# Residual norms of a two-model block stack taken token tile by token tile

## The chip, the cores and the metric

One core of one Trainium2 chip runs the program. The metric is the device time of one execution in microseconds (us), the median over several executions. The engines are called TensorE (PE; PEld is its weight load), VectorE (DVE), ScalarE (ACT), GpSimd (POOL) and SyncE (SP, which issues the transfers).

## The reference

Two models run one after the other on 256 tokens of width 1024 in fp32, two layers each. The first is a conditioned block with three mixers and a convolutional feed-forward network; its output x is the second one's input. The second model is the one whose norms are changed:

```python
for l in range(DEPTH):                                   # DEPTH = 2
    h = rms_norm_2(x, norm_mix_pre[l])
    (c_q, c_kv, k_rope, ..., gate_logits) = split(h @ w_in[l], pts)
    y_a = mla_branch(c_q, c_kv, k_rope, ...) @ w_o_mla[l]  # norms c_q and c_kv first
    ...
    merged = g[:, :, 0] * y_a + g[:, :, 1] * y_b + g[:, :, 2] * y_c + g[:, :, 3] * y_d
    x = x + rms_norm_2(merged @ w_out[l], norm_mix_post[l])
    h2 = rms_norm_2(x, norm_ffn_pre[l])
    f_g, f_u = split(h2 @ w_ffn_in[l])
    f = (silu(f_g) * f_u) @ w_ffn_out[l]
    x = x + rms_norm_2(f, norm_ffn_post[l])
```

`rms_norm_2(x, g)` divides each row by the root of its mean square (plus 1e-6) and multiplies by g. So a residual of the second model takes two norms in a row: of the product that is added, and of the sum for the next product.

## The kernel before

The 256 tokens are two token tiles t0 and t1 of 128 rows. A product's weights come from memory in pieces of 128x1024 fp32 (`raw`), and `weights` splits each piece into a high half `wh` (a cast on ACT, L259) and a low half `wl` (a subtraction on DVE, L260). Every product is three matmuls (`mm3`, L178 to L180): high by high, high by low, low by high. Activations are split in the same way (L262 on ACT, L263 on DVE when a gain is applied). A scheduler decides in which order each engine's instructions stand; each engine then works strictly in that order. `queue` adds an order without a wait for data. The table `HOLD` says, per norm ("site"), how many weight pieces may be split freely before the norm's last splits and how many stand behind them.

The second model has five places at which a residual ends: gpre of layer 0 (the first model's feed-forward product `down`, L868, gated and added, then normed as input of layer 0), gffn of layer 0 (product with w_out, `out_proj`, L1240), gpre of layer 1 (product with w_ffn_out, `down`, L1325), gffn of layer 1, and the end, where x goes out (L1399). The four accumulators of such a product, two halves cc of 512 columns for each token tile, lie in PSUM banks named acc, acc (t0) and ada, o (t1). The product runs in groups of two row blocks: for each group t0's four products (two row blocks by two halves), then t1's.

`add_normed` (L1350) takes the sums of squares of all four halves on ACT (L216), multiplies by the gain (L1361, DVE), computes the reciprocal root per token tile (`rsqrt`, L189 to L202, small DVE steps), adds to x (L1366, DVE, twice per tile) and sums the squares of the new x on ACT. `normed` (L219) takes the second reciprocal root, scales x (L232 on DVE for the left half, L233 on ACT for the right) and transposes it on PE, eight 128x128 blocks per token tile (L236), into four banks that both token tiles share; `norm_split` then splits the transposed blocks.

Behind gpre come the latent products (`lat`, banks acc, 24 matmuls of 512 columns per token tile), the product of the rope key (`krp`, 48 matmuls of 256 columns), the latents' own norm (sums of squares on ACT, a four-column Newton chain L189, L207 to L211 and scalings L1027 on DVE), its transposes (L1034, PE) and the rope key's own steps L1014 and L1015 (DVE). Behind gffn comes the feed-forward network: 22 hidden tiles of 128, each with 48 matmuls of 256 columns (weights stationary, tokens moving), Silu on ACT (L1339) and a product on DVE (L1340), and every two hidden tiles one group of `down`.

## Time and profile before

| what | value |
|---|---|
| median of 3 runs | 2169.36 us (2168.35 to 2172.04) |
| the profiled execution's own time | 2168.22 us |
| its span in the trace | 2166.4 us |
| PE busy | 2081.5 us, 96% of the span, 14228 matmuls |
| DVE busy | 1493.9 us, 69% |
| ACT busy | 1075.5 us, 50% |
| read from HBM | 328.2 MB, 152 GB/s over the span |
| mean granted PE clock | 0.978 of full speed |

The span is the stretch from the first to the last instruction of the profiled execution; the time beside it has some 1.8 us around it. All times in the rows below count from the span's start. An idle time in brackets behind a row is the engine's idle time just before it, with the instruction that ended it; a busy time of a group of "x8" is for all eight together.

### The profile page before, as it was taken

The numbers are of one execution on the slowest core, as the hardware profiler recorded it, in microseconds if no ns is written. First come the engines' busy times: TensorE is split into PE (matmuls) and PEld (weight loads), VectorE is DVE, ScalarE is ACT, GpSimd is POOL, SyncE is SP. The second block draws the span as 40 slices with busy tenths as digits, with TensorE's granted clock in tenths as the row PEclk, the third lists the DMA queues.
The fourth block names the chain that finished last, engine by engine and source line by source line (L and its number), as shares of the span: only waits on it lengthen the run. The fifth ranks groups of instructions, "written<-read, shape, count | busy, mean of one in ns | idle before, by whom it ended". The sixth has DMA issues, their size and how long they took to land.

```text
span 2166.4 us, 35861 instructions
## 1 busy us (share of the span) xinstructions
PE 2081.5 (96%) x14228; PEld 1850.0 (85%) x14228; DVE 1493.9 (69%) x3008; ACT 1075.5 (50%) x1837; POOL 0.8 (0%) x7
## 2 busy tenths in 40 slices
PE   6999999899999999989999999989998999998998
PEld 3886859688888898879997899979997899997997
DVE  5664666755555688687778799775556879876554
ACT  4545552542424366656556644454445644454443
POOL 0000000000000000000000000000000000000000
PEclk9999999899999999999999999999999999999999
DMA  8345563414142321145553555645553455654552
GB/s 341 122 164 180 202 218 116 156 58 146 55 138 67 128 89 55 39 135 199 197 190 132 165 178 182 196 156 171 189 185 123 156 166 163 197 187 139 188 183 72
DMA packets 94840, 331.65 MB, mean 153 GB/s; under 512 B 10928, under 2 KB 11312, under 8 KB 94544
## 3 DMA queue, kind: packets, MB, share of 16 engines
q1 hardware_dynamic: 94672, 329.35, 45.8%
q8 instruction: 112, 1.84, 0.3%
q14 instruction: 56, 0.46, 0.1%
HBM read 328.20 MB, written 1.11 MB: 152 GB/s over the span
## 4 chain that ended last, share of the span: by engine, by line
PE 90%; DVE 6%; ACT 2%; DMA 1%; issue 1%; DVEq 0%; ACTq 0%
PE ps L178 17%; PE ps L179 17%; PE ps L180 17%; PE acc L178 6%; PE acc L179 6%; PE acc L180 6%; PE ada L318 3%; PE ps L525 2%; PE o L566 2%; PE ps L550 2%; PE ada L180 1%; PE ada L178 1%; PE ada L179 1%; PE o L178 1%; PE o L179 1%; PE o L180 1%
## 5 line engine op out<-in xcount | busy, mean ns | idle before, releaser
L178 PE MATMUL ps<-T,wh 128*128 128x256 f32 (+1 forms) x2640 | 787.6, 299 | 1.1 <-ACT T L262 1.1
L179 PE MATMUL ps<-T,wh 128*128 128x256 f32 (+1 forms) x2640 | 785.6, 298 | 0.4 <-DVE T L263 0.4
L180 PE MATMUL ps<-T,wl 128*128 128x256 f32 (+1 forms) x2640 | 784.6, 298 | 0.0
L260 DVE TENSOR_TENSOR wl<-wraw,wh 128x1024 fp32r<-128x1024 f32 (+1 forms) x514 | 608.5, 1200 | 151.0 <-ACT wh L259 83.7
L259 ACT CAST wh<-wraw 128x1024 fp32r<-128x1024 f32 (+1 forms) x514 | 515.9, 1032 | 236.7 <-PE ps L179 77.3
L178 PEld LDWEIGHTS ps<-T,wh 128*128 128x128 f32 x2640 | 506.2, 192 | 18.5 <-ACT T L262 2.2
L179 PEld LDWEIGHTS ps<-T,wh 128*128 128x128 f32 x2640 | 506.5, 192 | 17.3 <-DVE T L263 1.2
L180 PEld LDWEIGHTS ps<-T,wl 128*128 128x128 f32 x2640 | 506.2, 192 | 13.7
L178 PE MATMUL acc<-wh,T 128*128 128x256 f32 (+1 forms) x988 | 314.9, 320 | 4.3 <-ACT T L265 3.1
L179 PE MATMUL acc<-wl,T 128*128 128x256 f32 (+1 forms) x988 | 313.6, 318 | 1.9 <-DVE wl L260 1.9
L180 PE MATMUL acc<-wh,T 128*128 128x256 f32 (+1 forms) x988 | 312.0, 317 | 0.3 <-DVE T L269 0.3
L178 PEld LDWEIGHTS acc<-wh,T 128*128 128x128 f32 x988 | 191.5, 194 | 20.9 <-ACT T L265 3.5
L180 PEld LDWEIGHTS acc<-wh,T 128*128 128x128 f32 x988 | 190.7, 193 | 14.6 <-DVE arena L268 1.7
L179 PEld LDWEIGHTS acc<-wl,T 128*128 128x128 f32 x988 | 191.4, 194 | 13.0 <-DVE wl L260 2.4
L1132 DVE SCALAR_TENSOR_TENSOR arena<-arena 128x241 f32<-128x241 f32 (+14 forms) x240 | 113.1, 473 | 3.7
L259 ACT CAST T<-arena 128x256 fp32r<-128x256 f32 (+2 forms) x128 | 58.8, 468 | 96.2 <-PE ps L179 25.8
L534 DVE TENSOR_REDUCE arena<-ps 128x1 f32<-128x512 f32 (+1 forms) x100 | 67.0, 683 | 44.9 <-PE ps L525 44.5
L318 PE MATMUL ada<-wraw,arena 128*32 128x512 f32 x384 | 86.5, 622 | 11.0 <-DVE arena L293 8.4
L1340 DVE TENSOR_TENSOR arena<-arena,ps 128x256 f32<-128x256 f32 x44 | 18.5, 421 | 113.8 <-ACT arena L1339 113.8
L260 DVE TENSOR_TENSOR T<-arena,T 128x256 fp32r<-128x256 f32 (+2 forms) x128 | 63.1, 500 | 48.6 <-ACT T L259 48.2
L698 ACT ACTIVATE arena<-ps,arena 128x512 f32<-128x512 f32 (+1 forms) x88 | 58.8, 669 | 74.6 <-PE ps L180 74.6
L1339 ACT ACTIVATE arena<-ps 128x256 f32<-128x256 f32 x44 | 16.9, 384 | 156.4 <-PE ps L180 156.4
(226 smaller groups left out, 2316.1 us busy)
## 6 DMA issues: line engine op xcount, KB each, us to landing
wraw<-w SPq DMA_DIRECT2D x586, 512.0 KB, 4.1
wraw<-w SPq DMA_DIRECT2D x22, 256.0 KB, 3.4
xo<-row SPq DMA_DIRECT2D x12, 256.0 KB, 5.7
v<-xin SPq DMA_DIRECT2D x4, 512.0 KB, 7.9
arena<-rpb SPq DMA_DIRECT2D x8, 256.0 KB, 3.5
v<-post SPq DMA_DIRECT2D x4, 512.0 KB, 4.0
arena<-bada SPq DMA_DIRECT2D x6, 256.0 KB, 6.9
arena<-bc SPq DMA_DIRECT2D x2, 768.0 KB, 4.0
```

The lines of the kernel that those rows point to most:

```text
L178: mm(out, ah, bh, start=start, stop=False)
L179: mm(out, ah, bl, start=False, stop=False)
L180: mm(out, al, bh, start=False, stop=stop)
L259: a = nc.scalar.copy(h, src)
L260: b = nc.vector.tensor_tensor(l, src, h.bitcast(F32), op=ALU.subtract)
L318: nc.tensor.matmul(ps[32 * g : 32 * g + 32, :], self.cT[:, k].rearrange("p s r -> p (s r)"), raw[g // 2][0][:, g % 2 * 512 : g % 2 * 512 + ...
L525: self.nc.tensor.matmul(ps[:, col : col + 256], a[:, c], b, start=(n == 0), stop=(n == len(q[s]) - 1))
L534: nc.vector.tensor_reduce(m, ps.rearrange("p (t k) -> p t k", t=nt), axis=AX, op=ALU.max, negate=True)
L550: nc.tensor.transpose(ps[:, b * P : b * P + P], p[:, b * P : b * P + P], K.ident)
L566: self.nc.tensor.matmul(out[64 * i : 64 * i + 64, t * P : t * P + P], v[:, k, cols[i] : cols[i] + 64], pts[i][:, b * P : b * P + P], start ...
L698: nc.scalar.activation(y[:, :n], ps[:, :n], AF.Identity, scale=cw[:, j, 1:2], bias=self.sm["cb"][:, j : j + 1])
L1132: yield v.scalar_tensor_tensor(y[:, lo:hi], zs[j][:, lo + t - 15 : hi + t - 15], self.cfw[:, j, t : t + 1], y[:, lo:hi], op0=ALU.mult, op1 ...
```

## The change

The change takes the two norms of a residual one token tile at a time. `norm_tile` (new) does for one token tile what `norm_to` does for both, into two banks of its own, and `add_normed` now returns a function `residual(t)` that does the gain, the root, the addition and the sums of squares of one token tile; the sum of squares of the second half of x is a DVE instruction with an accumulator (new L1403) instead of one on ACT. By `queue`, t1's second gain product and its first root stand behind t0's scaling of x. `rows` (new) orders a residual's product by token tile: the last four row blocks form one group, t0's 24 matmuls ahead of t1's, and within the last two row blocks the left half is finished before the right. The latent products of t0 stand ahead of t1's norm.

In the feed-forward network the first two hidden tiles are computed with the tokens stationary and 256 weight columns moving, per token tile: 48 matmuls of 256 columns for each, 96 as before. Their result has tokens in rows, so that four 128x128 transposes per layer (new L1350) bring it to columns. In the second model the split weights have eight buffers each (wh2, wl2) instead of five, out of the same shared slots, and `HOLD` lets no piece go free at both sites and puts the next six behind split number 15. x goes out in four transfers of 256 KB (new L1398) instead of two of 512 KB. The diff, cut to its core:

```diff
-HOLD = dict(n11=(4, 6, 7), n20=(2, 6, 7), n21=(4, 6, 7), gpre=(2, 6, 7), gffn=(4, 6, 7))
+HOLD = dict(n11=(4, 6, 7), n20=(2, 6, 7), n21=(4, 6, 7), gpre=(0, 6, 15), gffn=(0, 6, 15))
...
+    BUFS = dict(T=20, xo=5, wraw=5, wh=5, wl=5, wh2=8, wl2=8, v4=3)
...
+            h, l = (self.wide(tag, F32R) for tag in self.wtags)
...
+    def norm_tile(self, x, t, sums, dst, gain, site):
+
+        nc = self.nc
+        r = self.rsqrt(sums or [self.sumsq(x[:, c : c + 512]) for c in (0, 512)], 1, 1.0 / D)
+        xn = self.xo()
+        self.scaled = nc.vector.tensor_scalar(xn[:, :512], x[:, :512], r, None, op0=ALU.mult)
+        nc.scalar.activation(xn[:, 512:], x[:, 512:], AF.Copy, scale=r)
+        c = slice(t * P, t * P + P)
+        for k4 in range(0, KD, 4):
+            ps = self.bank()
+            for k in range(4):
+                nc.tensor.transpose(ps[:, k * P : k * P + P], xn[:, (k4 + k) * P : (k4 + k + 1) * P], self.ident)
+            for k in range(4):
+                h, l = dst[k4 + k]
+                ins = self.split(ps[:, k * P : k * P + P], h[:, c], l[:, c], gain[:, k4 + k : k4 + k + 1])
+                self.hold(site, t * KD + k4 + k, ins)
+
+    def rows(self, acc, flat, key, layer, X, a, n, last):
+
+
+        get = [self.weights(flat, key, layer, a + i, 2, [0], 1024) for i in range(0, n, 2)]
+        order = [(f, cc) for f in range(n - 2) for cc in range(2)] + [(f, cc) for cc in range(2) for f in (n - 2, n - 1)]
+        for t in range(2):
+            c = slice(t * P, t * P + P)
+            for f, cc in order:
+                h, lo = X[a + f]
+                self.mm3(acc[t, cc], (h[:, c], lo[:, c]), get[f // 2](f % 2 * 1024 + cc * 512, 512), a + f == 0, a + f == last - 1)
...
+                if j % 2 == 1 and 3 <= j < FT - 1:
+                    K.rows(ps, f"w1_{l}", "w_down", l, F, j - 3, 2, FT)
+            K.rows(ps, f"w1_{l}", "w_down", l, F, FT - 4, 4, FT)
...
-        K.norm_to(x, H, 0, sm["gpre"], sums=self.sums, site="gpre", tiles=((0,), (1,)))
...
+        lat = [None, None]
         get = [K.weights(wname, "w_in_2", l, u, 4, [0], 512) for u in range(0, KD, 4)]
         for t in range(2):
+            K.norm_tile(x[t], t, self.residual(t), H, sm["gpre"], "gpre")
+            lat[t] = K.bank("acc")
...
-        K.norm_to(x, H, 0, sm["gffn"], sums=sums, site="gffn")
+        get = [K.weights(wname, "w_ffn_in_2", l, 0, KD, [c], 256) for c in (0, FT * P)]
+        residual = self.add_normed(acc, 0)
+        ft = None
+        for t in range(2):
+            K.norm_tile(x[t], t, residual(t), H, sm["gffn"], "gffn")
+            ps = K.bank()
+            for i in range(2):
+                for k in range(KD):
+                    h, lo = H[k]
+                    K.mm3(ps[:, i * 256 : i * 256 + 256], (h[:, t * P : t * P + P], lo[:, t * P : t * P + P]), get[i](k * 256, 256), k == 0, k == KD - 1)
+            s = K.tmp()
+            act(s[:, :256], ps[:, :256], AF.Silu)
+            v.tensor_tensor(s[:, 256:], s[:, :256], ps[:, 256:], op=ALU.mult)
+            ft = ft or K.bank()
+            for j in range(2):
+                nc.tensor.transpose(ft[:, j * 256 + t * P : j * 256 + t * P + P], s[:, 256 + j * P : 256 + j * P + P], K.ident)
...
+        hv = self.halves(2)
+        for j in range(2):
+            F[j] = hv[j]
+            K.split(ft[:, j * 256 : j * 256 + 256], *F[j])
...
+        def residual(t, last=False):
+            parts, tm, sums = [], [], []
             for cc in range(2):
+                parts.append(K.sumsq(acc[t, cc]))
                 tm.append(K.tmp())
-                v.tensor_tensor(tm[cc], acc[t, cc], gain[:, cc * 512 : cc * 512 + 512], op=ALU.mult)
-            r = K.rsqrt(parts[t], 1, 1.0 / D)
-            out = []
+                ins = v.tensor_tensor(tm[cc], acc[t, cc], gain[:, cc * 512 : cc * 512 + 512], op=ALU.mult)
+                if t and cc and not last:
+                    K.queue(ins, K.scaled)
+            r = K.rsqrt(parts, 1, 1.0 / D, after=K.scaled if t and not last else None)
             for cc in range(2):
-                xc = self.x[t][:, cc * 512 : cc * 512 + 512]
+                c = slice(cc * 512, cc * 512 + 512)
+                xc = self.x[t][:, c]
                 v.scalar_tensor_tensor(xc, tm[cc], r, xc, op0=ALU.mult, op1=ALU.add)
-                if more:
-                    out.append(K.sumsq(xc))
-            sums.append(out)
-        return sums
+                if last:
+                    nc.sync.dma_start(self.ap["out"][t * P : t * P + P, c], xc)
+                elif cc == 0:
+                    sums.append(K.sumsq(xc))
+                else:
+                    out = K.small(1)
+                    v.scalar_tensor_tensor(K.tmp(), xc, 1.0, xc, op0=ALU.mult, op1=ALU.mult, accum_out=out)
+                    sums.append(out)
+            return sums
+
+        return residual
```

Three places of the order show what moves. On DVE at gffn of layer 0 (acc are t0's accumulators, ada and o t1's two; L1366 adds to x, L232 scales it), before:

```order
L1361 TENSOR_TENSOR arena<-ada_14137,v_1678_14283 128x512
L1366 SCALAR_TENSOR_TENSOR arena<-arena 128x512 x2
L1361 TENSOR_TENSOR arena<-o_14138,v_1678_14283 128x512
L189 TENSOR_SCALAR arena<-arena 128x1 x2
L191 SCALAR_TENSOR_TENSOR arena<-arena 128x1 x2
...
L202 SCALAR_TENSOR_TENSOR arena<-arena 128x1 x2
L1366 SCALAR_TENSOR_TENSOR arena<-arena 128x512 x2
L232 TENSOR_SCALAR xo_14321<-arena 128x512
```

and with the change (L1389 is the gain product, L1396 the addition, L1403 the sum of squares, L257 the scaling):

```order
L1396 SCALAR_TENSOR_TENSOR arena<-arena 128x512 x2
L1403 SCALAR_TENSOR_TENSOR arena<-arena 128x512
L189 TENSOR_SCALAR arena<-arena 128x1
L1389 TENSOR_TENSOR arena<-ada_14137,v_1694_14311 128x512
L191 SCALAR_TENSOR_TENSOR arena<-arena 128x1
L189 TENSOR_SCALAR arena<-arena 128x1
...
L204 SCALAR_TENSOR_TENSOR arena<-arena 128x1
L257 TENSOR_SCALAR xo_14337<-arena 128x512
L1389 TENSOR_TENSOR arena<-o_14138,v_1694_14311 128x512
L191 SCALAR_TENSOR_TENSOR arena<-arena 128x1
```

Before, both token tiles' first roots stand paired ahead of t0's scaling; now t0's scaling L257 stands ahead of t1's second gain product, with t1's first gain product still in between.

On DVE behind gpre of layer 1 (L189, L207 to L211 is the latents' Newton chain, L1027 scales the latents, L1014 needs the rope key's products, ps_16413), before:

```order
L209 TENSOR_TENSOR arena<-arena 128x4
L260 TENSOR_TENSOR wl_16528<-wraw_16523,wh_16527 128x1024
L210 SCALAR_TENSOR_TENSOR arena<-arena 128x4
L211 SCALAR_TENSOR_TENSOR arena<-arena 128x4
L209 TENSOR_TENSOR arena<-arena 128x4
L210 SCALAR_TENSOR_TENSOR arena<-arena 128x4
L211 SCALAR_TENSOR_TENSOR arena<-arena 128x4
L1027 TENSOR_SCALAR arena<-acc_16337,arena 128x256 x2
L1027 TENSOR_SCALAR arena<-acc_16338,arena 128x256 x2
L260 TENSOR_TENSOR wl_16532<-wraw_16525,wh_16531 128x1024
L1014 TENSOR_TENSOR arena<-ps_16413,arena 128x512
```

and with the change (L211 to L213 are the chain's steps, L1037 and L1038 the rope key's, L1050 scales the latents):

```order
L290 TENSOR_TENSOR wl_2000_16730<-wraw_16725,wh_1999_16729 128x1024
L1037 TENSOR_TENSOR arena<-ps_16434,arena 128x512
L213 SCALAR_TENSOR_TENSOR arena<-arena 128x4
L290 TENSOR_TENSOR wl_2002_16734<-wraw_16727,wh_2001_16733 128x1024
L1038 TENSOR_TENSOR arena<-arena 128x256
L211 TENSOR_TENSOR arena<-arena 128x4
L212 SCALAR_TENSOR_TENSOR arena<-arena 128x4
L213 SCALAR_TENSOR_TENSOR arena<-arena 128x4
L211 TENSOR_TENSOR arena<-arena 128x4
L212 SCALAR_TENSOR_TENSOR arena<-arena 128x4
L213 SCALAR_TENSOR_TENSOR arena<-arena 128x4
L1050 TENSOR_SCALAR arena<-acc_16329,arena 128x256 x2
```

The rope key's L1037 and L1038 and two weight splits (L290, two more stand above these rows, behind L189) now stand ahead of the chain's last steps and of the scalings.

On PE at gffn of layer 0 (xo is the scaled x), before, where the last row is the first hidden tile's first product:

```order
L236 MATMUL ps_14326<-arena,xo_14321 128x128 x2
L236 MATMUL ps_14323<-arena,xo_14322 128x128 x2
...
L236 MATMUL ps_14326<-arena,xo_14322 128x128 x2
L178 MATMUL ps_14395<-T_14317,wh_14387 128x256
L178 MATMUL ps_14461<-T_14317,wh_14453 128x256
L179 MATMUL ps_14395<-T_14317,wh_14387 128x256
```

and with the change (ps_14366 takes t0's products of the first two hidden tiles, L263 is the transpose of the scaled x, ps_14473 takes t1's products):

```order
L180 MATMUL ps_14366<-wh_1692_14307,T_14286 128x256
L1350 MATMUL ps_14417<-arena 128x128 x2
L263 MATMUL ps_14447<-arena,xo_14444 128x128 x4
L263 MATMUL ps_14460<-arena,xo_14444 128x128 x4
L178 MATMUL ps_14473<-wh_1684_14291,T_14283 128x256
L179 MATMUL ps_14473<-wl_1685_14292,T_14283 128x256
```

Before, t1's transposes follow t0's at once; now 48 products of t0 and two transposes of their result (L1350) stand between.

## Rows read from the trace of the kernel before

**Rows 1.** The page's chain that ended last, by engine (share of the span).

```profile
PE 90%; DVE 6%; ACT 2%; DMA 1%; issue 1%; DVEq 0%; ACTq 0%
```

**Rows 2.** PE's waits: line waited for: us in total, times, longest us.

```profile
PE ps L236 <- DVE xo L232: 21.9, 9, 6.9
```

**Rows 3.** Timeline, PE, gffn of layer 0: start us, us, engine line op, [idle before <-releaser].

```profile
1451.67 0.39 PE L179 MATMUL o<-wl,T 128*128 128x512 f32 x1
...
1451.90 0.39 PE L180 MATMUL o<-wh,T 128*128 128x512 f32 x1
...
1459.53 1.97 PE L236 MATMUL ps<-arena,xo 128*128 128x128 f32 x8 [7.24 <-DVE arena L189]
```

**Rows 4.** Windows: from:to us, busy of each engine (instructions), PEclk, DMA share, GB/s.

```profile
1155.00:1158.10 3.10, 2.65 (x16) 2.42 (x17) 1.67 (x8) 1.73 (x5) 0.00 (x0) 0.67 0.01 5
...
1459.50:1464.00 4.50, 3.50 (x15) 3.10 (x16) 2.04 (x10) 2.01 (x5) 0.00 (x0) 0.50 0.32 83
...
1468.00:1472.00 4.00, 4.00 (x35) 4.00 (x35) 3.50 (x3) 2.26 (x4) 0.00 (x0) 1.00 0.38 129
```

**Rows 5.** Timeline, DVE, gffn of layer 0.

```profile
1449.65 0.69 DVE L1361 TENSOR_TENSOR arena<-acc,v 128x512 f32<-128x512 f32 x1 [7.30 <-ACT arena L216]
...
1457.66 1.41 DVE L1366 SCALAR_TENSOR_TENSOR arena<-arena 128x512 f32<-128x512 f32 x2
...
1458.99 0.48 DVE L232 TENSOR_SCALAR xo<-arena 128x512 f32<-128x512 f32 x1
...
1477.42 0.42 DVE L1340 TENSOR_TENSOR arena<-arena,ps 128x256 f32<-128x256 f32 x1 [1.41 <-ACT arena L1339]
```

**Rows 6.** Lines L216 and L233, ACT: duration ns min/median/max, first and last start us.

```profile
L216 ACT ACTIVATE arena<-acc x8: 597/598/598, 1448.9 to 2154.4; 128x512 f32<-128x512 f32 x8
...
L216 ACT ACTIVATION_READ_ACCUMULATOR arena<-acc x8: 194/194/195, 1449.4 to 2154.9; 128x1 f32 x8
...
L233 ACT ACTIVATE xo<-arena x16: 708/722/723, 10.2 to 1966.3; 128x512 f32<-128x512 f32 x16
```

**Rows 7.** Timeline, DVE, gpre of layer 0: splits of 128 columns.

```profile
1157.68 1.91 DVE L263 SCALAR_TENSOR_TENSOR T<-ps,arena,T 128x128 fp32r<-128x128 f32 x6 [1.19 <-ACT T L262]
```

**Rows 8.** Timeline, PE, gpre of layer 0 and of layer 1.

```profile
1155.06 1.10 PE L236 MATMUL ps<-arena,xo 128*128 128x128 f32 x8 [3.87 <-DVE xo L232]
...
1175.54 1.03 PE L1034 MATMUL ps<-arena 128*128 128x128 f32 x8
...
1658.46 1.97 PE L236 MATMUL ps<-arena,xo 128*128 128x128 f32 x8 [6.24 <-DVE arena L189]
...
1674.54 0.28 PE L178 MATMUL ps<-T,wh 128*128 128x256 f32 x1
...
1680.29 0.93 PE L1034 MATMUL ps<-arena 128*128 128x128 f32 x7
```

**Rows 9.** Timeline, DVE, latent chain of layer 1.

```profile
1675.64 0.17 DVE L189 TENSOR_SCALAR arena<-arena 128x4 f32<-128x4 f32 x1
...
1676.75 1.23 DVE L260 TENSOR_TENSOR wl<-wraw,wh 128x1024 fp32r<-128x1024 f32 x1
...
1678.94 1.66 DVE L1027 TENSOR_SCALAR arena<-acc,arena 128x256 f32<-128x256 f32 x4
...
1681.65 0.69 DVE L1014 TENSOR_TENSOR arena<-ps,arena 128x512 f32<-128x512 f32 x1
```

**Rows 10.** Timeline, PE and DVE, the end of the program.

```profile
2156.63 0.39 PE L180 MATMUL o<-wh,T 128*128 128x512 f32 x1
...
2158.51 0.68 DVE L1361 TENSOR_TENSOR arena<-ada,v 128x512 f32<-128x512 f32 x1
...
2159.71 0.14 DVE L189 TENSOR_SCALAR arena<-arena 128x1 f32<-128x1 f32 x1
...
2161.37 1.41 DVE L1366 SCALAR_TENSOR_TENSOR arena<-arena 128x512 f32<-128x512 f32 x2
```

**Rows 11.** The page's DMA issues: count, KB each, us to landing.

```profile
out<-arena SPq DMA_DIRECT2D x2, 512.0 KB, 2.6
```

More of the change, by code (lines that the diff above doesn't have):

```diff
@@ L62, in __init__ @@
         self.filler = None
+        self.wtags = "wh", "wl"
         self.specs = {}
@@ L180, in mm3, with rsqrt @@
         mm(out, al, bh, start=False, stop=stop)
-    def rsqrt(self, parts, n, inv_n):
+    def rsqrt(self, parts, n, inv_n, after=None):
         v = self.nc.vector
@@ L190, in rsqrt @@
             else:
-                v.scalar_tensor_tensor(x, p, inv_n * big, x, op0=ALU.mult, op1=ALU.add)
+                ins = v.scalar_tensor_tensor(x, p, inv_n * big, x, op0=ALU.mult, op1=ALU.add)
+                if after:
+                    self.queue(ins, after)
         a, b = self.small(n), self.small(n)
@@ L866, in layer @@
             ps = dict(zip([(t, cc) for t in tts for cc in range(2)], K.acc4()))
-            def down(a):
-                get = K.weights(f"w1_{l}", "w_down", l, a, 2, [0], 1024)
-                for t in tts:
-                    for f in range(2):
-                        h, lo = F[a + f]
-                        for cc in range(2):
-                            K.mm3(ps[t, cc], (h[:, t * P : t * P + P], lo[:, t * P : t * P + P]), get(f * 1024 + cc * 512, 512),
-                                  a + f == 0, a + f == FT - 1)
             F = {}
@@ L879, in layer, with residual @@
                 F[j] = self.ffn_up(l, j, XT, n)
-                if j % 2 == 1 and j >= 3:
-                    down(j - 3)
-            down(FT - 2)
-            for t in tts:
+                if j % 2 == 1 and 3 <= j < FT - 1:
+                    K.rows(ps, f"w1_{l}", "w_down", l, F, j - 3, 2, FT)
+            K.rows(ps, f"w1_{l}", "w_down", l, F, FT - 4, 4, FT)
+            def residual(t):
                 for cc in range(2):
                     self.add_gated(self.x[0][t][:, cc * 512 : cc * 512 + 512], ps[t, cc], gates[0][:, cc * 512 : cc * 512 + 512])
+            self.residual = residual
 class Block2:
@@ L891, in __init__ @@
         self.depth = depth
-        self.sums = None
         self.nc = K.nc
@@ L991, in layer @@
         H = self.halves(KD)
-        K.norm_to(x, H, 0, sm["gpre"], sums=self.sums, site="gpre", tiles=((0,), (1,)))
-        lat = [K.bank("acc") for _ in range(2)]
+        lat = [None, None]
         get = [K.weights(wname, "w_in_2", l, u, 4, [0], 512) for u in range(0, KD, 4)]
         for t in range(2):
+            K.norm_tile(x[t], t, self.residual(t), H, sm["gpre"], "gpre")
+            lat[t] = K.bank("acc")
             for k in range(KD):
@@ L1238, in layer @@
         acc = {}
-        def out_proj(u):
-            get = K.weights(wname, "w_out_2", l, u, 2, [0], 1024)
-            for t in range(2):
-                for k in range(2):
-                    h, lo = M[u + k]
-                    for cc in range(2):
-                        K.mm3(acc[t, cc], (h[:, t * P : t * P + P], lo[:, t * P : t * P + P]), get(k * 1024 + cc * 512, 512),
-                              u + k == 0, u + k == KD - 1)
         YC = self.halves(4)
@@ L1344, in layer, with add_normed @@
             K.split(s[:, 256:], *F[j])
-            if j % 2 == 1 and j >= 3:
-                down(j - 3)
-        down(FT - 2)
-        self.sums = self.add_normed(acc, 1, more=l < self.depth - 1)
-    def add_normed(self, acc, which, more=True):
+            if j % 2 == 1 and j < FT - 1:
+                K.rows(acc, wname, "w_ffn_out_2", l, F, j - 3, 2, FT)
+        K.rows(acc, wname, "w_ffn_out_2", l, F, FT - 4, 4, FT)
+        self.residual = self.add_normed(acc, 1)
+        if l == self.depth - 1:
+            for t in range(2):
+                self.residual(t, last=True)
+    def add_normed(self, acc, which):
         K, nc = self.K, self.nc
@@ L1395 @@
         b1.layer(l)
+    b2.residual = b1.residual
+    K.wtags = "wh2", "wl2"
     for l in range(d2):
         b2.layer(l)
-    for t in range(2):
-        nc.sync.dma_start(ap["out"][t * P : t * P + P, :], x[t])
     specs.update(K.specs)
```

22 lines of the change are left out of this document (4 added, 18 removed).

## The prediction

> **What bounds the kernel now.** I read the chain of waits first: TensorE (PE) carries 90% of the time that sets the end, VectorE (DVE) 6%, ScalarE (ACT) 2% [rows 1]. So only two things move the end: fewer PE columns, or shorter stretches in which PE stands still. The change keeps the columns (four extra 128x128 transposes per layer apart), so everything is decided in the stretches. PE's own waits name them: the largest entry is the transposes of the row norms at L236, 21.9 us for L232, the scaling of x, one of the nine waits 6.9 us long [rows 2]. The long ones lie where a residual of the second model is added and normed. At the norm ahead of the FFN of layer 0 (gffn) the last product starts at 1451.90 and the first transpose at 1459.53: 7.24 us of nothing [rows 3]. I call the end of the last product e (1452.29 there: its start plus 0.39) and count from it. Matmuls of 512 columns start 0.23 us apart [rows 3]. The granted clock is at its lower level, 0.50, over the transposes that follow, 0.67 in the mean at the norm of layer 0's input (gpre, behind the first model), and 1.00 again in the stretch that begins 4 us after the first products at gffn [rows 4].
>
> **gffn, twice.** Products now go t0 first: of the last four row blocks all 24 matmuls of t0, then 24 of t1. So t0's accumulators are done 24 x 0.225 = 5.4 us ahead of e, its first half 6.75 ahead. What follows on DVE and ACT costs what it cost: gain product L1361 0.68, residual L1366 0.74 each [rows 5], sum of squares on ACT 0.60 plus 0.19 for the read of its accumulator, scaling L233 0.72 [rows 6], rsqrt chain 1.66 (from L189 at 2159.71 to the L1366 at 2161.37 [rows 10]), L232 0.48 [rows 5]. In order: sum of squares to e-4.3, rsqrt to e-2.5, two residuals to e-1.1, last sum of squares to e-0.35. This last one now is a DVE instruction with an accumulator (L1403 of the new kernel). No row shows such an instruction on DVE; it lies between L1366's 0.74, the same shape, and 0.74 + 0.19 with a read like ACT's [rows 5, 6]. I take 0.8; the ends shift each chain by 0.1.
>
> The Trainium skill (VectorE: DVE Perf Modes, section "Two Vector instructions with no wait between them") counts such an operation as two instructions, the main one and a read of the accumulator; that speaks for the upper end, and by it each gffn would gain 0.1 to 0.2 us less. No row of the kernel before shows it.
>
> Behind it DVE's order puts t1's first gain product ahead of the second rsqrt (+0.68), then rsqrt 1.66 and L257 0.48: the first transposes of t0 at about e+2.8 instead of e+7.24. The gain is not 4.4 us, for t0's products are then fed by 8 pairs of splits of 128 columns, six of which took 1.91 us on DVE [rows 7], and these stand in one queue with t1's chain: 0.68 + 1.6 + 1.5 + 0.8 + 1.6 + 0.48 = 6.7 us. So the 48 products of t0 (5.8 us at 0.12, like the 48 between 1674.54 and 1680.29 [rows 8]) end at about e+12.9, not at e+9. Then PE's next row is the new transposes L1350, which wait for Silu and product (0.42 [rows 5], and about as much for Silu) and stand ahead of t1's transposes: about 1.05 of stall; t1's transposes and first split to e+15.7, 48 products to e+21.4. Before, the same 96 products end at e+24.6: the product L1340 of the second hidden tile starts at 1477.42 [rows 5], behind its Silu. That is -3.2. Against it: four transposes 0.25, a second, shorter wait at L1350 0.4, and 0 to 2 for PE at the lower clock while it is fed thinly (before, it runs full behind its first product). I take **-1.7 each, -3.4 for both**, ends 0 and -3.
>
> **gpre, layer 1.** The same t0-first order, so the latent products (L, 24 per token tile) end at e+18.6 to 19.3. Before they end at 1674.54, with e = 1652.22 (6.24 us before the transposes, which are at 1658.46): e+22.3. So 3.5 us are won at L. But see what is late next. Behind the latent products PE has 48 products of the rope key (5.75 us, from 1674.54 to 1680.29) and then at once the transposes L1034 of the normed latents [rows 8]. Those need DVE's chain L189 to L1027, which before runs under these 48 products: it starts at 1675.64, has one weight cast in it (1.23), and ends with L1027 at 1680.60; only then come L1014 and L1015, which need the rope key products [rows 9]. In the new order three casts stand between the steps of that chain ahead of L1037 (the old L1014), and a fourth behind it, and L1037 itself stands ahead of the last seven steps. L1037 can't start before the 48 products end, at L + 5.75. From there DVE has 0.68, 0.16, cast 1.22, L1038 some 0.4 (half of L1037's columns), six steps of 0.2, four scalings 1.66 [rows 9]: 5.3 us, some 4.7 with the overlap of starts. PE's next row is the transposes, so it idles for that: they come at about e+29.0, where before they come at e+28.07. What is won back is 0.7, since L1014 and L1015 no longer stand between the splits behind. Net **+0.2**, ends -3.5 (no stall) and +1.5.
>
> **gpre, layer 0.** Behind the first model t0 gains less: the last hidden tile's product waits for the convolution, so that t0's accumulators are done only some 3.7 us ahead of e, and the gated additions of both token tiles are four products and four sums on DVE, three of t1's within t0's rsqrt. First transposes at about e+4.0, 3.9 before [rows 8]; L at e+17.9 against e+18.7. And the same DVE order behind it: before, L1034 starts at 1175.54, right at the end of the rope key products [rows 8]; now 4.7 us later than their end. -0.8 + 4.7 + 0.9 for the queued casts ahead of the chain - 0.7 = **+4.1**, ends -0.8 and +5.
>
> **The end.** Before, DVE does both L1366 of t0 before the gain products of t1, so these start 1.5 us late (2158.51, the last product being done at 2156.63 + 0.39 = 2157.02), then rsqrt and two L1366 [rows 10]. Now t0 is finished while PE still works on t1: two L1366 (1.4) leave the path. The result goes out in four transfers of 256 KB, each behind its half. One of 512 KB takes 2.6 us to landing [rows 11]; 256 KB lies between 1.3 and 2.6, I take 2.3, near the upper end, since the last of four queues behind the third. **-1.7**, ends -1 and -2.5.
>
> **Covered.** Four weight casts come ahead of each norm (HOLD 0 instead of 2 or 4): DVE stands idle for 7.30 us ahead of the first L1361 [rows 5], four casts take 4.9, so nothing; if they were late, L1389 stands behind them, 1.2 us each. The norm's weights stay in 8 buffers instead of 5: nothing either, for the slots are shared in both kernels. Two new stalls of 5 us let the clock fall as in [rows 4]: +0.6 for both.
>
> **Sum.** -3.4 + 0.2 + 4.1 - 1.7 + 0.6 = -0.2 us. The profiled run took 2168.2, 1.1 below the median of 2169.36; against the median I forecast **2169 us**. Differences under 0.2% (4.3 us) can't be told from none; so faster means under 2165.0, slower over 2173.7.
>
> **Rivals.**
> *The stall of DVE's latent chain does not come* (the casts were done early, or L1037 waits for less): then gpre gives -0.8 and -3.5, and the sum is -0.8 - 3.5 - 3.4 - 1.7 = -9.4: 2160. For it: DVE is 69% busy only, and the chain before ended 0.3 us past the products. Against it: L1037 stands in the queue, and it reads the last of 48 products. Chance 0.30.
> *The clock stays low* (slower). PE is used thinly where t0's products wait for splits. If the granted clock is 0.50 when t1's products start and stays there, 48 products cost 5.8 and 24 latent ones 5.4 more, 22.4 over four norms; it decides once it lasts for over a third of them. Before, the 4.5 us of transposes were at 0.50, and PE is at 1.00 again from 1468 [rows 4], 4 us into full products; so half of it at most, 11 less the 2 counted above: 2178. Chance 0.12. The Trainium skill (TensorE: Matmul & The Clock Gate, "Loop structure matters more than you think") says that the order of the loop decides whether TensorE keeps its rate, and that a long wait between products drops it. That speaks against this order of products, and [rows 4] agree: 0.50 behind 7.24 us of idling.
> *The change doesn't do what it says*: t0's norm is no earlier in effect, since t1's chain fills DVE between t0's splits, and gffn gains nothing: +3.4, 2172.6. Chance 0.18.
> The forecast itself: 0.40.
>
> **How the numbers follow.** Faster: most of the first rival (0.26) and the lower tail of the forecast (0.06): 0.32. Slower: the clock (0.12), 0.06 of the forecast's upper tail, 0.05 of the third: 0.23. Same: 0.45. The range goes from 2159, which takes in the first rival, to 2176, which leaves out most of the clock's case; about 0.15 to 0.2 is outside. The forecast's own range is 2164 to 2174.
>
> **What would show it.** Right: at both gffn first transposes at e+2.5 to 3.5 and PE's second batch of transposes 10 us later; at both gpre an idle stretch of PE of 4 to 6 us ahead of the transposes of the latents, put down to the scaling L1050; a tail of 7.7 us from the last product to the end (9.4 before). Wrong: no such stretch (first rival); clocks of 0.5 to 0.7 over t1's products (second).

## The result and the profile after

The changed kernel takes 2185.12 us (median of 4 runs, 2182.75 to 2187.86); the kernel before took 2170.29 us beside it. The ratio is 1.0069, 95% interval 1.0056 to 1.0082: slower by 14.8 us, where 2169 was forecast and 2159 to 2176 given.

The time is best read in stages that end with the last product ahead of a residual's norm, which is where the transposes' idle time begins. The timeline of PE after gives these points (start of the first transpose less the idle time in brackets); they answer to [rows 3, 8]:

```profile
1160.16 1.21 PE L263 MATMUL ps<-arena,xo 128*128 128x128 f32 x8 [3.69 <-DVE arena L199]
...
1471.60 1.76 PE L263 MATMUL ps<-arena,xo 128*128 128x128 f32 x7 [2.46 <-DVE xo L257]
...
1669.42 1.85 PE L263 MATMUL ps<-arena,xo 128*128 128x128 f32 x8 [2.38 <-DVE xo L257]
...
1982.56 1.09 PE L263 MATMUL ps<-arena,xo 128*128 128x128 f32 x8 [2.46 <-DVE xo L257]
```

Before, the fourth point is in this row of PE's timeline:

```profile
1964.38 1.97 PE L236 MATMUL ps<-arena,xo 128*128 128x128 f32 x8 [7.33 <-DVE arena L189]
```

| stage, us in the profiled execution | before | after | moved |
|---|---|---|---|
| mixing, layer 0 (gpre, branches, w_out) | 301.1 | 312.7 | +11.6 |
| feed-forward, layer 0 | 199.9 | 197.9 | -2.0 |
| mixing, layer 1 | 304.8 | 313.1 | +8.2 |
| feed-forward, layer 1 | 200.0 | 198.4 | -1.6 |
| tail behind the last product | 9.4 | 7.2 | -2.2 |

That is +14.0, close to the 14.8 us between the medians; each stage value comes from one execution. The profiled span itself grew by 19.3 us; 5.3 of it lie ahead of the first point, in the first model, most of it in its first 50 us, where PE waits 5.6 us for the first weights instead of 2.6. The medians, 14.8 us apart, hardly show that part.

So the feed-forward stages and the tail won 5.8 us, close to the forecast, and the mixing stages lost more than three times as much. PE's waits after show where to look first; they answer to [rows 2]:

```profile
PE ps L1057 <- DVE arena L1050: 9.2, 2, 4.9
...
PE ps L263 <- DVE xo L257: 7.3, 3, 2.5
...
PE ps L263 <- DVE arena L199: 3.7, 1, 3.7
...
PE ps L178 <- ACT arena L1275: 3.7, 8, 1.0
```

The waits for the scaled x sum to 11.0 us in four places now (second and third row). Before, they were 27.2 us behind the first model, most of it in this row, which [rows 2] does not show:

```profile
PE ps L236 <- DVE arena L189: 20.8, 3, 7.3
```

Of the 21.9 us of [rows 2], 15.5, with the wait of 6.9 us, belong to the first model's norms and not to the second's, as the prediction read it; nothing in its sum hangs on that. New after the change are 9.2 us at the transposes of the latents and eight short waits for ACT's gate L1275. DVE's timeline at gpre of layer 0 shows the first of them; the rows answer to [rows 9]:

```profile
1176.81 0.16 DVE L189 TENSOR_SCALAR arena<-arena 128x4 f32<-128x4 f32 x1
...
1177.11 1.22 DVE L290 TENSOR_TENSOR wl<-wraw,wh 128x1024 fp32r<-128x1024 f32 x1
...
1178.33 1.22 DVE L290 TENSOR_TENSOR wl<-wraw,wh 128x1024 fp32r<-128x1024 f32 x1
...
1179.54 1.22 DVE L290 TENSOR_TENSOR wl<-wraw,wh 128x1024 fp32r<-128x1024 f32 x1
...
1180.74 1.22 DVE L290 TENSOR_TENSOR wl<-wraw,wh 128x1024 fp32r<-128x1024 f32 x1
...
1181.88 0.68 DVE L1037 TENSOR_TENSOR arena<-ps,arena 128x512 f32<-128x512 f32 x1
...
1182.55 1.22 DVE L290 TENSOR_TENSOR wl<-wraw,wh 128x1024 fp32r<-128x1024 f32 x1
...
1184.80 0.16 DVE L213 SCALAR_TENSOR_TENSOR arena<-arena 128x4 f32<-128x4 f32 x1
...
1185.00 1.66 DVE L1050 TENSOR_SCALAR arena<-acc,arena 128x256 f32<-128x256 f32 x4
```

and PE's row there, which answers to [rows 8]:

```profile
1185.54 2.33 PE L1057 MATMUL ps<-arena 128*128 128x128 f32 x8 [4.92 <-DVE arena L1050]
```

Four casts of 1.22 us stand inside a chain of small steps ahead of L1037, a fifth behind it. The rope key's products had ended at 1180.62; PE waited 4.92 us. The windows of that stall, of the transposes behind it, of the first products behind these and of t1's products at gffn read:

```profile
1180.62:1185.54 4.92, 0.00 (x1) 0.01 (x1) 4.75 (x14) 0.10 (x1) 0.00 (x0) 0.94 0.89 302
1185.54:1188.40 2.86, 2.32 (x8) 1.50 (x8) 1.60 (x4) 0.97 (x3) 0.00 (x0) 0.50 0.00 1
1188.40:1192.00 3.60, 3.57 (x13) 3.24 (x14) 2.64 (x5) 1.95 (x4) 0.00 (x0) 0.54 0.00 0
1483.00:1487.00 4.00, 3.93 (x22) 2.75 (x21) 2.59 (x8) 3.06 (x9) 0.00 (x0) 1.00 0.00 0
```

The granted clock is 0.50 over the transposes behind the stall, which last 2.33 us instead of 1.03 [rows 8], 0.54 over the next 3.60 us of products, and 1.00 over t1's products at gffn. The second loss goes with waits of ACT's casts and of the transfers' issuer SP behind the first model (the first row from 1160 us on, the others from 1200 to 2100 us):

```profile
ACT wh L289 <- DMA wraw<-w: 37.9, 27, 3.2
...
SPq L145 <- DVE wl L290: 251.6, 95, 8.9
...
SPq L145 <- PE ps L180: 309.7, 125, 6.3
```

Before, no cast waits for a transfer there, and SP's rows are:

```profile
SPq L144 <- PE ps L180: 445.3, 156, 11.4
SPq L144 <- DVE wl L260: 122.2, 54, 5.1
```

Now 27 casts wait for their raw weights. The transfers wait twice as long for a split (L260, now L290), but less for a product: the two rows sum to 567.5 us before and 561.3 after. So SP hardly waits longer in all (790 and 802 us over all its rows); it waits more often for a slot that a split frees and less often for one that a product frees. That transfers of raw weights wait for products at all, which read only the split halves, fits slots that are shared.

### The profile page after: what moved, and what is told of

Its sections match the earlier page's. It is cut to its first block, busy times and chain, and to the rows that moved or that the text cites. A ratio compares the mean times of both kernels' runs of the same rounds, so it can differ in the third digit from the quotient of the medians.

```text
span 2185.7 us, 35937 instructions
## 1 busy us (share of the span) xinstructions
PE 2097.4 (96%) x14236; PEld 1855.9 (85%) x14236; DVE 1505.5 (69%) x3036; ACT 1083.0 (50%) x1841; POOL 0.8 (0%) x7
## 4 chain that ended last, share of the span: by engine, by line
PE 85%; DVE 7%; ACT 3%; DMA 2%; issue 2%; DVEq 0%; ACTq 0%; SPq 0%
PE ps L178 16%; PE ps L179 15%; PE ps L180 15%; PE acc L178 6%; PE acc L179 6%; PE acc L180 6%; PE ada L348 3%; DMA wraw<-w 2%; PE ps L555 2%; DVE wl L290 2%; PE o L596 2%; PE ps L580 2%; PE o L180 1%; PE o L179 1%; PE ada L179 1%
## 5 line engine op out<-in xcount | busy, mean ns | idle before, releaser
L290 DVE TENSOR_TENSOR wl<-wraw,wh 128x1024 fp32r<-128x1024 f32 (+1 forms) x514 | 611.5, 1202 | 273.3 <-ACT wh L289 66.1
L178 PE MATMUL ps<-T,wh 128*128 128x256 f32 (+1 forms) x2576 | 771.3, 300 | 4.8 <-ACT arena L1275 3.7
L179 PE MATMUL ps<-T,wh 128*128 128x256 f32 (+1 forms) x2576 | 767.6, 298 | 0.0
L180 PE MATMUL ps<-T,wl 128*128 128x256 f32 (+1 forms) x2576 | 765.0, 298 | 0.0
L289 ACT CAST wh<-wraw 128x1024 fp32r<-128x1024 f32 (+1 forms) x514 | 521.2, 1031 | 374.9 <-PE ps L179 100.7
L178 PEld LDWEIGHTS ps<-T,wh 128*128 128x128 f32 x2576 | 494.2, 192 | 25.8 <-ACT arena L1275 8.4
L179 PEld LDWEIGHTS ps<-T,wh 128*128 128x128 f32 x2576 | 494.1, 192 | 16.2 <-DVE T L299 0.9
L180 PEld LDWEIGHTS ps<-T,wl 128*128 128x128 f32 x2576 | 493.0, 192 | 14.0
L178 PEld LDWEIGHTS acc<-wh,T 128*128 128x128 f32 x988 | 191.9, 195 | 21.9 <-ACT T L295 3.5
L728 ACT ACTIVATE arena<-ps,arena 128x512 f32<-128x512 f32 (+1 forms) x88 | 58.7, 669 | 72.3 <-PE ps L180 72.3
L290 DVE TENSOR_TENSOR T<-arena,T 128x256 fp32r<-128x256 f32 (+2 forms) x124 | 61.1, 503 | 45.9 <-ACT T L289 45.2
L568 ACT ACTIVATE arena<-ps,arena 128x512 f32<-128x512 f32 (+1 forms) x120 | 73.4, 619 | 29.8 <-DVE arena L564 22.4
L731 DVE SCALAR_TENSOR_TENSOR arena<-ps,arena 128x510 f32<-128x510 f32 (+1 forms) x88 | 53.9, 613 | 41.3 <-ACT arena L728 41.3
```

The source lines that it names most:

```text
L178: mm(out, ah, bh, start=start, stop=False)
L179: mm(out, ah, bl, start=False, stop=False)
L180: mm(out, al, bh, start=False, stop=stop)
L289: a = nc.scalar.copy(h, src)
L290: b = nc.vector.tensor_tensor(l, src, h.bitcast(F32), op=ALU.subtract)
L568: nc.scalar.activation(p[:, c], ps[:, c], AF.Exp, bias=m[:, i : i + 1], accum_out=tot[:, i : i + 1])
```

## The experiments

Theory A was that the place of the casts and of L1037 in DVE's queue costs; B, that the eight buffers of the split weights do; C and D, that the new order of products itself does. All were taken with the kernel before beside them (its medians 2170.2 to 2170.8 us). The stages are from each run's profiled execution.

| run | median us | ratio to before (95%) | mixing 0, 1 | feed-forward 0, 1 |
|---|---|---|---|---|
| change | 2185.1 | 1.0069 (1.0056 to 1.0082) | 312.7, 313.1 | 197.9, 198.4 |
| e1_buf5 | 2178.0 | 1.0040 (1.0026 to 1.0055) | 304.4, 306.4 | 202.2, 202.2 |
| e2_hold | 2184.4 | 1.0066 (1.0048 to 1.0084) | 311.0, 311.6 | 198.4, 199.7 |
| e3_krlate | 2183.9 | 1.0060 (1.0044 to 1.0077) | 312.3, 314.2 | 197.5, 197.7 |
| e4_buf5hold | 2181.0 | 1.0051 (1.0034 to 1.0068) | 307.2, 306.4 | 202.5, 202.3 |
| e5_tags | 2161.6 | 0.9958 (0.9944 to 0.9973) | 300.7, 300.7 | 198.8, 198.2 |
| e6_before8 | 2185.1 | 1.0067 (1.0052 to 1.0082) | 311.1, 314.0 | 197.9, 197.9 |
| e7_tagsffn | 2175.6 | 1.0029 (1.0017 to 1.0040) | 300.7, 300.6 | 206.1, 207.0 |
| e8_tagssq | 2160.2 | 0.9948 (0.9934 to 0.9963) | 300.7, 300.6 | 198.7, 198.3 |
| e9_tagshold | 2173.3 | 1.0015 (1.0006 to 1.0025) | 304.2, 303.7 | 201.1, 201.3 |
| e10_tagsgroup | 2172.3 | 1.0009 (1.0000 to 1.0019) | 300.7, 304.1 | 202.2, 201.8 |
| e11_buf6 | 2181.6 | 1.0044 (1.0030 to 1.0059) | 308.2, 308.8 | 201.4, 200.7 |
| e12_fence | 2171.7 | 1.0007 (0.9997 to 1.0016) | 306.3, 307.4 | 197.9, 199.7 |

### Buffers, holds and L1037, one at a time

```diff
-    BUFS = dict(..., wh2=8, wl2=8, v4=3)
+    BUFS = dict(..., wh2=5, wl2=5, v4=3)
```

> Five buffers each for the split weights of the second model instead of eight; nothing else of the change is taken back. Theory A (only the place of L1037 and of the casts in DVE's queue costs): in this order one cast instead of four is in the latent chain, and L1037 stands behind the first of the four scalings; the idle stretch of PE ahead of the latents' transposes falls from 4.9 and 4.3 us to about 2.5 each, the casts' waits for transfers (27 behind 1200 us, 38 us in sum) stay, and the time is about 2179. Theory B (the eight buffers take slots from the raw weights, so that casts wait for transfers and ACT's gate L1275 behind them comes late): these waits go as well, PE's waits for L1275 (3.7 us) with them, 2172 to 2175. Theory C (products by token tile leave PE thin and slow): nothing moves, 2183 to 2187.

Half of the loss goes: the mixing stages win 8.3 and 6.7 us, PE's stretch ahead of the latents' transposes falls to 2.0 and 1.4 us, and no cast waits for a transfer any more. But the feed-forward stages lose 4 us each. Their first transposes come 5.5 us behind the last product instead of 2.46, since casts (L290) now stand on DVE in the norm's own chain. At gffn of layer 0 the first of three stands ahead of these rows, and the last product ends at 1457.64:

```profile
1456.11 0.75 DVE L1396 SCALAR_TENSOR_TENSOR arena<-arena 128x512 f32<-128x512 f32 x1
1456.78 1.22 DVE L290 TENSOR_TENSOR wl<-wraw,wh 128x1024 fp32r<-128x1024 f32 x1
1457.91 0.74 DVE L1396 SCALAR_TENSOR_TENSOR arena<-arena 128x512 f32<-128x512 f32 x1
1458.64 1.22 DVE L290 TENSOR_TENSOR wl<-wraw,wh 128x1024 fp32r<-128x1024 f32 x1
1459.79 0.69 DVE L1403 SCALAR_TENSOR_TENSOR arena<-arena 128x512 f32<-128x512 f32 x1
```

So eight buffers serve the norm ahead of the feed-forward network, whose casts are done early with them, and harm the mixing stage. That the early casts need the eight buffers was not looked at in the prediction.

```diff
-HOLD = dict(..., gpre=(0, 6, 15), ...)
+HOLD = dict(..., gpre=(2, 6, 7), ...)
```

> Only the hold of gpre goes back to (2, 6, 7), eight buffers stay. Theory A: one cast in the latent chain and L1037 behind two of the four scalings: PE's idle stretch falls to about 2 us in each layer, about 2178. Theory B: the casts' waits for transfers and PE's waits for L1275 stay as they are (3.7 us), so that no more than the stretches' 5 us and 1 to 2 us of low clock are won: 2177 to 2180. Theory C: 2183 to 2187.

PE no longer idles for 5 us ahead of the latents' transposes (1.7 us in four pieces over both layers), and yet only 1.6 and 1.5 us are won; the median is within the noise of the change's. Every reading but C forecast 5 us or more; C's 2183 to 2187 holds this run and the next, and only e5_tags and e6_before8 below rule it out. The first transposes of gpre come later, 5.0 and 4.2 us instead of 3.7 and 2.4; e9_tagshold below gives a price for this hold.

```diff
-        v.tensor_tensor(kr, krp, self.rope[:, 512:], op=ALU.mult)
...
             ln.append(o)
...
+        K.queue(v.tensor_tensor(kr, krp, self.rope[:, 512:], op=ALU.mult), normed)
```

> Only the rope key's two steps L1037 and L1038 are put behind the four scalings of the latents; the four casts stay in the chain, as do holds and buffers. If L1037 is what costs in the stretch: PE idles for at most 1.5 us ahead of the latents' transposes, and 6 to 8 us are won, 2177 to 2179. If the four casts (1.22 each) fill the chain by themselves: the stretch is still some 3 to 4 us, and 1 to 3 us are won, 2182 to 2184. Theory C: 2183 to 2187.

PE still waits 4.0 and 3.4 us ahead of the latents' transposes: the casts fill the chain by themselves, and L1037, which I had named, is worth 0.9 us of it. The median moves by 1.2 us, within the noise.

The first two edits together:

```diff
-HOLD = dict(..., gpre=(0, 6, 15), ...)
+HOLD = dict(..., gpre=(2, 6, 7), ...)
...
-    BUFS = dict(..., wh2=8, wl2=8, v4=3)
+    BUFS = dict(..., wh2=5, wl2=5, v4=3)
```

> Both: five buffers and the hold of gpre as before. Theory A and B together: stretch of PE about 2 us in each layer, no casts that wait for transfers behind 1200 us: 2171 to 2174. Theory B alone: like five buffers alone, within 1.5 us. Theory C: 2183 to 2187.

Slower than five buffers alone by 3.0 us, though the intervals overlap: the old hold of gpre costs in layer 0 (304.4 to 307.2 us) and gains nothing in layer 1 (306.4 in both). The expectation of 2171 to 2174 missed, since it left out what five buffers cost ahead of the feed-forward network.

### Where the buffers matter

```diff
+        K.wtags = "wh", "wl"
         ((w, _),) = K.raw(wname, "w_kr_2", l, 0, KD, [0], 64)
...
+        K.wtags = "wh2", "wl2"
         for u in range(0, KD - 4, 2):
             K.rows(acc, wname, "w_out_2", l, M, u, 2, KD)
```

> The whole change, but the eight buffers serve only from the product with w_out to the latent products; between the latent products and w_out (the mixing stage) the split weights have the five buffers of before. Theory B (eight buffers in the mixing stage put the casts too far ahead: into the latent chain, and ahead of the gates while their raw weights are still on the way): the mixing stages go from 312.7 and 313.1 us to 302 to 306 and 298 to 304, the stages with the feed-forward network stay at 198, the casts no longer wait for transfers behind 1200 us, and the time is 2163 to 2168, below the kernel before. Rival D (the products by token tile themselves slow the mixing stage): mixing stages of 308 or more, 2172 to 2180.

2161.6 us, 0.42% faster than the kernel before (0.27 to 0.56) and a little under the 2163 to 2168 expected. In PE's timeline the first transposes come as early as with the change, and the latents' transposes (first row) follow the rope key's products without a wait:

```profile
1178.22 1.04 PE L1058 MATMUL ps<-arena 128*128 128x128 f32 x8
...
1457.26 1.09 PE L263 MATMUL ps<-arena,xo 128*128 128x128 f32 x8 [2.46 <-DVE xo L257]
...
1656.29 1.18 PE L263 MATMUL ps<-arena,xo 128*128 128x128 f32 x8 [2.69 <-DVE xo L257]
...
1956.80 1.31 PE L263 MATMUL ps<-arena,xo 128*128 128x128 f32 x8 [2.46 <-DVE xo L257]
```

DVE's latent chain of layer 0 has no cast in it, and L1038 (the rope key) stands behind the scalings:

```profile
1174.57 0.16 DVE L189 TENSOR_SCALAR arena<-arena 128x4 f32<-128x4 f32 x1
...
1176.74 1.66 DVE L1051 TENSOR_SCALAR arena<-acc,arena 128x256 f32<-128x256 f32 x4
...
1179.45 0.68 DVE L1038 TENSOR_TENSOR arena<-ps,arena 128x512 f32<-128x512 f32 x1
```

SP waits for splits even less than before, and no cast waits for a transfer:

```profile
SPq L145 <- DVE wl L290: 78.9, 59, 5.7
```

```diff
-    BUFS = dict(..., wh=5, wl=5, v4=3)
+    BUFS = dict(..., wh=5, wl=5, wh2=8, wl2=8, v4=3)
...
+    K.wtags = "wh2", "wl2"
     for l in range(d2):
```

> The kernel before with eight buffers each for the split weights of the second model, and nothing else of the change. Theory B: both mixing stages get 7 to 11 us longer, with an idle stretch of PE of 3 to 5 us ahead of the latents' transposes (three casts and L1014 stand in the chain in this order) and casts that wait for transfers; 2183 to 2192. Rival D (the loss comes with the new order of products and norms): 2167 to 2174.

The kernel before with eight buffers and nothing else of the change is as slow as the change. Its waits, of PE (first two rows) and of ACT behind the first model:

```profile
PE ps L1034 <- DVE arena L1027: 5.5, 2, 2.8
...
PE ps L178 <- ACT arena L1261: 3.0, 8, 0.9
...
ACT wh L259 <- DMA wraw<-w: 37.7, 27, 3.2
```

The wait for L1027 is the stall ahead of the latents' transposes (2.8 and 2.7 us, a little less than the 3 to 5 expected), L1261 is the gate. The mixing stages are 10.0 and 9.2 us longer than before. This rules out C and D as the cause of the loss: no new order of products or norms is in this kernel.

The same run shows something that I had put down to the new order. The feed-forward stages, in the old order, win 2.0 and 2.1 us with eight buffers alone, as much as with the change. The first transposes at gffn of layer 0 come earlier than the 7.24 us of [rows 3], and no cast stands in the norm's chain any more, where one of 1.22 us stood before:

```profile
1469.52 1.97 PE L236 MATMUL ps<-arena,xo 128*128 128x128 f32 x8 [6.25 <-DVE arena L189]
```

So with eight buffers throughout, the new order wins nothing in the feed-forward stages, and only the tail (9.5 us here, 7.2 with the change) is its own gain there. How much of the 8.7 us by which e5_tags is below the kernel before comes without the new order is open: the kernel before with eight buffers only from w_out to the latent products was not run.

The change with six buffers:

```diff
-    BUFS = dict(..., wh2=8, wl2=8, v4=3)
+    BUFS = dict(..., wh2=6, wl2=6, v4=3)
```

> The whole change with six buffers each instead of eight, in all of the second model. If raw weights are starved step by step as the split halves take slots: mixing stages between those of e1_buf5 (304 to 306) and of the change (313), casts that wait for transfers some 5 to 15 times behind 1200 us, feed-forward stages of 199 to 202, 2176 to 2182. If only the eighth pair tips it: mixing stages as with five, feed-forward stages as with eight, 2166 to 2172.

Between five and eight, in steps: the mixing stages at 308 us, PE's stall ahead of the latents' transposes 2.7 and 2.2 us. No cast waits for a transfer yet, where the first reading had 5 to 15, so these waits begin above six, and the mixing stages are 7.5 and 8.1 us longer than in e5_tags without them.

```diff
+        K.fence, K.pieces, K.free, K.held = (sq, normed), 0, 0, 4
         KT = []
```

This takes the change as it is, with L1037 as in e3_krlate; `normed` is the last scaling of the latents, `sq` ACT's last square of them.

> The whole change with eight buffers and its new holds, but the four further casts and the rope key's two steps are queued behind the scalings of the latents, so that the latent chain is as free as with five buffers. If the stall and the slower clock behind it are the larger part of the mixing stages' loss (12 us each against e5_tags): PE does not idle ahead of the latents' transposes, the mixing stages come to 304 to 307, the rest (casts that wait for transfers, some 25 times, and the gates L1275 behind them) stays, 2169 to 2174. If the four casts cost wherever they stand: 308 to 312, 2176 to 2182. If transfers that wait for splits are nearly all of it: 310 or more with no idle stretch.

2171.65 us. PE's first two rows here are the latents' transposes and the gates, the third is ACT's:

```profile
PE ps L1056 <- DVE arena L1046: 0.2, 1, 0.2
...
PE ps L178 <- ACT arena L1275: 4.8, 8, 2.4
...
ACT wh L289 <- DMA wraw<-w: 41.3, 29, 3.1
```

With the chain free the mixing stages win 6.4 and 5.7 us; the casts' waits stay and the stages remain 5.6 and 6.6 us longer than in e5_tags. So the loss has two parts of about equal size. The first is shown: casts in the latent chain, with the slow clock behind the stall. The second is weights that come late: on ACT, which works in order, a gate stands behind a cast that waits for its transfer, and PE waits for the gate. One such case in layer 1, on ACT (first two rows) and PE:

```profile
1898.85 1.04 ACT L289 CAST wh<-wraw 128x1024 fp32r<-128x1024 f32 x1 [2.95 <-DMA wraw<-w]
1899.80 0.47 ACT L1275 ACTIVATE arena<-ps,arena 128x256 f32<-128x256 f32 x1
...
1900.32 0.39 PE L178 MATMUL ps<-T,wh 128*128 128x256 f32 x1 [2.35 <-ACT arena L1275]
```

The gates' price is larger than the 4.8 us of PE's own waits, for PE's weight loads wait for them too. In the view of L1275 the loads of both layers' products wait

```profile
PEld ps L178: 9.6, 26
```

and in e5_tags, where the gate is L1276:

```profile
PEld ps L178: 1.0, 6
```

These waits overlap with PE's own. The 8.6 us between them are the larger part of the 12.2 us (5.6 and 6.6); what makes the rest is not shown.

### What the other parts are worth

These start from e5_tags. All 22 hidden tiles as before:

```diff
-        get = [K.weights(wname, "w_ffn_in_2", l, 0, KD, [c], 256) for c in (0, FT * P)]
...
         for t in range(2):
             K.norm_tile(x[t], t, residual(t), H, sm["gffn"], "gffn")
-            ps = K.bank()
...
-        for j in range(2, FT):
+        for j in range(FT):
```

> As e5_tags, but all 22 hidden tiles with the weights stationary as before: no products of t0 alone, no transposes of their result. If the early products of t0 carry the gain of the feed-forward stages: these go from 198 to 199 to 201 us, 2 to 5 us slower than e5_tags. If the gain comes from the norm's shorter chain alone: within 1.5 us of e5_tags.

The feed-forward stages take 206.1 and 207.0 us, 7 to 9 us more than in e5_tags and 6 to 7 more than before; the whole is 14.0 us slower, where 2 to 5 were expected. PE waits for t1's scaling with no products of t0 to do (6.9 and 6.5 us). But the edit changes a second thing: with the row-major tiles (the two whose result has tokens in rows) go the four weight pieces that were split ahead of the norm, and the hold puts the first hidden tile's pieces behind the norm's last split. PE waits for the first of them 3.94 us in each layer; in layer 0:

```profile
1470.79 0.58 PE L178 MATMUL ps<-T,wh 128*128 128x256 f32 x1 [3.94 <-ACT wh L289]
```

So the row-major tiles and the early split of their weights together carry the gain; without these two waits the stages would, by my estimate (206.1 and 207.0 less 3.94), still be 2 to 3 us longer than before.

With the last sum of squares on ACT:

```diff
-                elif cc == 0:
-                    sums.append(K.sumsq(xc))
                 else:
-                    v.scalar_tensor_tensor(K.tmp(), xc, 1.0, xc, op0=ALU.mult, op1=ALU.mult, accum_out=out)
+                    sums.append(K.sumsq(xc))
```

> As e5_tags, but the last sum of squares of x on ACT again instead of DVE. Price of L1403 as I took it (0.8 on DVE against 0.6 plus 0.19 on ACT behind the first one): within 1.5 us of e5_tags, 0.2 to 0.5 us slower or faster in each of four norms.

2160.2 us, all stages within 0.2 us: no difference that can be told. It is the fastest median of the study (0.9948), by less than the intervals.

With both holds as before:

```diff
-HOLD = dict(..., gpre=(0, 6, 15), gffn=(0, 6, 15))
+HOLD = dict(..., gpre=(2, 6, 7), gffn=(4, 6, 7))
```

> As e5_tags, with the holds of gpre and gffn as before, (2, 6, 7) and (4, 6, 7). If the new holds matter: casts get between the splits of t0 and t1 or ahead of the scaling; first transposes at gpre 1 to 2 us later as in e2_hold, at gffn up to 3 us; 2164 to 2170. If they don't: within 1.5 us of e5_tags, 2160 to 2163.

11.7 us slower, more than expected: first transposes 5.3, 6.4, 4.6 and 6.4 us behind the last product. The mixing stages lose 3.5 and 3.0 us. This price would account for e2_hold, whose hold takes most of the stall away and then costs some 3 us in front; it was taken with five buffers in the mixing stage, not with e2_hold's eight.

With the last four row blocks in two groups, at all three products (the one with w_out is shown):

```diff
-        K.rows(acc, wname, "w_out_2", l, M, KD - 4, 4, KD)
+        for u in (KD - 4, KD - 2):
+            K.rows(acc, wname, "w_out_2", l, M, u, 2, KD)
```

> As e5_tags, but the last four row blocks of a residual's product run in two groups of two, so that t0's accumulators are done 2.7 us ahead of the last product instead of 5.4. If t0's head start sets the wait: the first transposes come at 4 to 5 us behind the last product instead of 2.5, at gffn and at gpre of layer 1, and the time is 2165 to 2170. If DVE's order hides it (its chain of t1 holds t0 back anyway): within 1.5 us of e5_tags.

10.7 us slower, again more than expected; three of the four norms have their first transposes 5.2 to 5.4 us behind the last product. At gpre of layer 0 nothing moves (3.7 us): there DVE's queue has t1's gated products within t0's chain, and the last of them (L711 at 1153.99, after 0.18 us of idling) waits for the last product, as in e5_tags (at 1154.16, after 0.34 us).

## Why the prediction was wrong

- **The step that failed** stands under "Covered": "The norm's weights stay in 8 buffers instead of 5: nothing either, for the slots are shared in both kernels." This one edit makes the kernel before as slow as the change (e6_before8, 1.0067), and the change with eight buffers only around the norms is faster than before (e5_tags, 0.9958). With more buffers for the halves the casts stand earlier in the queues: on DVE in the latent chain, and on ACT ahead of the gates. That the slots are shared is no ground for a price of nothing: a raw piece takes one slot and its two halves take two, and after the change 27 casts wait for raw weights where none did.
- **The stall at the latents** was forecast from DVE's order, and its size (4.7 forecast, 4.92 and 4.30 measured) is right in part by luck. The prediction let L1037 start at the end of the rope key's products and counted 4.7 us from there; in layer 0 the casts ahead made it start 1.26 us later (1181.88), and the steps behind it took 3.66. The casts and not L1037 make the stall (e3_krlate), and that they stand there is again the buffers' doing (e1_buf5, e5_tags).
- **What follows the stall** was a mis-sized term: 0.6 us for both layers. The granted clock is 0.50 behind it, the transposes alone take 1.3 us longer, and the first products behind them run slowly too (0.54 over 3.60 us). In all, the free chain is worth 6.4 and 5.7 us (e12_fence) where the sum had 4.7 and 0.3 for the clock.
- **The rest of the mixing stages**, 5.6 and 6.6 us, was not in the sum at all. It goes when the five buffers come back there (e5_tags). Late weights, which make ACT's gates late, explain up to 8.6 of the 12.2 us (e12_fence); the remainder is open. This, the clock and the latents make +4.1 and +0.2 into +11.6 and +8.2.
- **gffn** came out as forecast in its steps: first transposes at e+2.46 (2.8 forecast), the wait at the new transposes 0.93 us (1.05). That -2.0 and -1.6 us also meet the -1.7 each is partly luck. The term stood for the order alone, with the buffers at nothing; yet the order with five buffers loses 2.3 and 2.2 us against the kernel before (e1_buf5), and the eight buffers alone win 2.0 and 2.1 in the old order (e6_before8). PE's row of that wait in layer 0:

```profile
1482.74 0.44 PE L1350 MATMUL ps<-arena 128*128 128x128 f32 x2 [0.93 <-DVE arena L1347]
```

- **The end** was right: 7.2 us (7.7 forecast), -2.2 us; with eight buffers in the old order it stays at 9.5.
- **The rivals.** "The stall does not come" is what e5_tags makes true: it forecast 2160 us, and 2161.6 were measured; but the condition was in the buffers, which the rival did not name. The clock over t1's products did not fall (1.00 in the window above), so the slower side came by another way than the rival I had priced. The third rival's mechanism did not come, since t0's transposes were early (e+2.46); but its outcome, an order that gains nothing at gffn, is what a comparison with e6_before8 gives (197.9 and 198.4 us against 197.9 twice).

## What to carry to other kernels

More buffers for one kind of tile in shared memory take depth from another kind: here casts ran ahead until 27 of them waited for raw weights, and a queue that works in order put them between the steps of a short chain. Give a deeper buffer only to the stretch that uses it, and read, for each edit to buffering, whose transfers or casts move and what stands behind them in the queue. A gain next to a loss shows in a table by stage, where the sum of the kernel hides both.

## What the runs showed of the hardware

An operation of DVE that also sums up its result is two instructions in the trace. The rows of L1403 (duration in ns, least, median and largest):

```profile
L1403 DVE SCALAR_TENSOR_TENSOR arena<-arena x6: 681/688/692, 1468.0 to 1987.3; 128x512 f32<-128x512 f32 x6
L1403 DVE DVE_READ_ACCUMULATOR arena<-arena x6: 80/82/85, 1468.7 to 1987.9; 128x1 f32 x6
```

Together 0.77 us, where I took 0.8 between 0.74 and 0.93. The Trainium skill (VectorE: DVE Perf Modes, "Two Vector instructions with no wait between them") says that such an operation is a main instruction and a read of the accumulator; the trace agrees. The read is 82 ns, under half of ACT's 0.19 [rows 6], so the upper end for which the prediction took this to speak did not come.

The clock behind a stall of PE: over the 4.92 us without products the granted clock was 0.94 in the mean, over the 2.86 us of transposes behind it 0.50, and over the next 3.60 us of products 0.54. Part of a stall's price falls due behind it.
